# A decoder step in split precision: ScalarE's work on loaded tiles kept in program order, decode steps and operand builds spread over each pair of M tiles

## The chip, the cores and the metric

The kernel runs on one core of a Trainium2 chip. The metric is the device time of one execution in microseconds (us), lower is better. The time before is the median of three runs.

## What is computed

One inference step of a two-layer trunk, for 512 prompt tokens and 8 sample tokens (one new token each, with a state of its own). All 520 tokens go through the same weights; the model width is 2048.

```python
h = rmsnorm(x, norm_g)
z = h @ w_in                       # 2048 -> 8192: B, C, xc, g_conv | q, k, v, g_ret, 1024 columns each
y_conv = B * conv3(C * xc) * silu(g_conv)                 # causal, width 3
q, k = rope(q), rope(k) / 16       # 4 heads of 256
o = retention(q, k, v, S0)         # decayed linear attention, chunks; new state S
y_ret = groupnorm(o) * gn_g * silu(g_ret)
x = x + concat(y_conv, y_ret) @ w_out
x = x + sigmoid(x @ w_pg) * (p @ w_ple)
# after the last layer: rmsnorm(x, final_g)
```

For the 8 sample tokens the retention is a decode step on a 256x256 state of each token and head: S = gamma * S + k^T v, o = q S. The new states are outputs as well. 2 layers x 4 heads x 8 tokens are 64 such steps.

## The kernel before

**Split precision.** Each fp32 operand is held as two parts of the type fp32r: a high part (a copy by ScalarE, line 222 for weights, line 527 for operands) and a low part (the rest, a subtraction by VectorE, lines 223 and 528). Each product is three matmuls, lines 240 to 242: high x high, high x low, low x high. The accumulators are PSUM banks of 260 columns, a half (LEFT or RIGHT) of the 520 tokens.

**Pairs of M tiles.** The four large products (w_in, w_out, w_pg, and w_in of the next layer) are done two M tiles of 128 rows at a time by pair(). For each pair a table (HEADS, CONVS, OUT_ROWS, GATES) gives a number s of the 16 K tiles that go through one step of Strassen's scheme (strassen(): 7 products instead of 8); the rest, from s to 16, is done plainly at the end. s = 0 means two plain products, one after the other (gemm()). In strassen() the products come in this order: `times(a, w11, k1)`, `times(b, w21, t1)`, `times(a, w21, t2)`, `times(d, w12, ...)`, then aside(), `times(a, w11, t3)`, `times(b, w21, ...)`, `times(a, w22, t4)`, then the plain rest, the last copies out of PSUM and a second aside(). Between the first four products VectorE adds weight tiles (line 305). ScalarE copies finished banks (line 293).

**Operands.** An Operands object (X, O, Gt: the input of w_in, w_out and w_pg) holds the split K tiles and, for the first s of them, four split sums per pair of tiles (sums, t1 to t4). build() makes those of one pair: a gain by ScalarE for X (line 455), operand_sums() on VectorE (lines 403 to 406), then split(). The tiles come from HBM through send(), one pair ahead of the build (AHEAD = 1), by the DMA queue of POOL (SIDE), line 1026 or 636. fill(most) builds at most `most` pairs, sending one ahead, as far as slots are free; supply(k) builds what a product needs at once. s grows over the first pairs of each product (0, 4, 8, 12, 14 or 4, 8, 12, 16), so sums must be made while pairs run. Before, MORE_HEAD = MORE_OUT = MORE_GATE = 2 builds are done at the end of each pair; MORE_CONV = 1 after each pair of the convolution stage. free() builds the next set's operands in the last pair of a product, as the old ones go.

**Retention.** head(m) runs a pair of q, k, v or g_ret tiles; steps(h) is a list s0 to s8 of small pieces for a head's prompt tokens, one of which is run at each aside(). two() (line 842) splits a tile that was loaded from scratch in HBM (hs). Decode steps are run by sample(): it finishes the step whose tiles were loaded in the call before (sample_step: ScalarE scales the state, line 747; VectorE adds two outer products, line 751, and reduces twice, line 755; POOL stores the state, line 752) and issues the loads of the next (sample_load: sret, line 741, and kq, line 742). In the head stage, sample() is called once after each pair, and twice after each second one (k and g_ret); in the convolution stage once before each pair.

**Order.** The program is written in one order, but a planner sets the order of each engine's queue: it simulates the run and issues on each engine, of the instructions that are ready by its own clock, the one that comes first in the program. Some stand ahead of their place by high_priority (PSUM copies, and by WPRIO = 20 places the weight splits). On the chip an engine takes its queue strictly as it was laid out. tc.keep_in_program_order(ins) adds an edge, without a wait, from the instruction that was written just before on the same engine: ins cannot be laid out ahead of that one; others can still pass.

Of the kernel before, what the change touches and what calls it, by code (L numbers as in the profile page):

```python
# [9 lines left out]
AF = mybir.ActivationFunctionType  # L10
# [32 lines left out]
RESERVE_NEXT = 10  # L43
AHEAD = 1
PRE = 9
MORE_HEAD, MORE_CONV, MORE_OUT, MORE_GATE = 2, 1, 2, 2
ROOT = (0, 3)
SPREAD = (0, 6)

# [138 lines left out]
def trunk_kernel(  # L188
# [19 lines left out]
    split_ring = Ring(const, SPLIT, F32R, "split")  # L208
    banks = Banks(pg, 5)
    later = []  # L210


    def load(src):
# [62 lines left out]
    def strassen(x, src0, src1, s, step=None):  # L276
# [70 lines left out]
        if c is None:  # L347
            plus(z1[:, RIGHT], a, z1[:, RIGHT])
        else:
            copy(z1[:, LEFT], a)  # L350
        times(b, w21, at(ops, k2, RIGHT), False, True)
        raw_ring.put(w21)
        step(6)
# [26 lines left out]
    def pair(x, src, m, n, nxt=None):  # L380


        s = x.rows[n]
        last = n == len(x.rows) - 1 and nxt is not None
        if s:
            z = strassen(x, src[m], src[m + 1], s, (lambda i: x.free(i, nxt)) if last else None)
        else:
            z0 = gemm(x, src[m], s)
            aside()
            z1 = gemm(x, src[m + 1], s)  # L390
            aside()
            z = z0, z1
            if last:
                x.free(8, nxt)
        x.release(n + 1)
        if nxt is not None and not last and not x.todo:
            nxt.fill(1, PRE)
        return z
# [14 lines left out]
    class Operands:  # L413
# [44 lines left out]
        def fill(self, most=KT, reserve=None):  # L458

            reserve = self.reserve if reserve is None else reserve  # L460
            while self.todo and self.todo[0][0] < self.ready:
# [8 lines left out]
                    continue  # L470
                break

        def supply(self, k):

            while self.todo and self.todo[0][1] and 2 * self.todo[0][0] < k:
                self.build()
# [44 lines left out]
    def split(src, g=None, free_src=True, halves=False, right=True):  # L521
        x, y = getr(), getr() if right else None
        op = Op(x, y, halves)
        for n in ((LEFT, RIGHT) if right else (LEFT,)) if halves else (slice(0, T),):
            hi, lo = op.view(n)
            if g is None:
                S.activation(hi, src[:, n], AF.Copy)  # L527
                V.tensor_tensor(lo, src[:, n], F(hi), SUB)  # L528
            else:
                S.activation(hi, src[:, n], AF.Identity, scale=g)  # L530
                V.scalar_tensor_tensor(lo, src[:, n], g, F(hi), MUL, SUB)  # L531
        if free_src:
            put(src)
        return op
# [153 lines left out]
    for l in range(DEPTH):  # L688
# [55 lines left out]

        def sample_step(h, b, st, kb):

            S.activation(st[:, :512], st[:, :512], AF.Identity, scale=gam(h))  # L747
            k = kb[:, 256:512]
            for e in range(2):
                c = slice(256 * e, 256 * e + 256)  # L750
                V.scalar_tensor_tensor(st[:, c], k, vs[:, h, e, b : b + 1], st[:, c], MUL, ADD)  # L751
            SIDE.dma_start(o_rets[l, h, b], st[:, :512])  # L752
            for e in range(2):
                c = slice(256 * e, 256 * e + 256)
                V.tensor_tensor_reduce(k, st[:, c], kb[:, :256], 1.0, 0.0, MUL, ADD, osum[:, e, h, b : b + 1])  # L755
            put(st, kb)
# [13 lines left out]
        skipped = 2 if l == 0 else 0  # L770

        def head(m):
            zs = pair(X, wi[l], m, m // 2 - skipped)
            X.fill(MORE_HEAD, 0)
            for _ in range(1 + m // 2 % 2):
                sample()
            return zs

        def aside_copy(h, i, tiles):
# [49 lines left out]
        def steps(h):  # L829
# [9 lines left out]

            def two(src, scale=1.0):  # L840
                hi, lo = getr(), getr()
                S.activation(hi[:, :512], src[:, :512], AF.Copy, scale=scale)
                if scale == 1.0:
                    V.tensor_tensor(lo[:, :512], src[:, :512], F(hi[:, :512]), SUB)
                else:
                    V.scalar_tensor_tensor(lo[:, :512], src[:, :512], scale, F(hi[:, :512]), MUL, SUB)
                return hi, lo
# [195 lines left out]
        for j in range(CJ):  # L1043
            mt = 32 + 4 * j
            O.ready = min(j // 2, 3)
            sample()
            zc, zx = pair(X, wi[l], mt, mt // 2 - skipped, O)
            u = get()
            times(u, zc, r2)
# [13 lines left out]
            put(u)  # L1063
            V.tensor_tensor(t, t, rb, MUL)
            X.fill(MORE_CONV, 0)
            sample()
            if j == CJ - 1:
                while loaded or todo:
                    sample()
# [26 lines left out]
        for m in range(0, KT, 2):  # L1096
            xs = [get(), get()]
            for i in range(2):
                SIDE.dma_start(xs[i], res[m + i])
            Gt.ready = m // 2  # L1100
            zs = pair(O, wo[l], m, m // 2, Gt)
            for i, (x, z) in enumerate(zip(xs, zs)):
                for n, v in z:
                    V.tensor_tensor(x[:, n], v, x[:, n], ADD)
                z.done()
                SIDE.dma_start(x1s[l, m + i], x)
                if m < SPILL_X:
                    put(x)
                else:
                    x1[m + i] = x  # L1110
            O.fill(MORE_OUT, 0)


        pops = []
# [24 lines left out]
        for m in range(0, KT - tail, 2):  # L1139
            pes, xs = [], [again(x1s, m), again(x1s, m + 1)]  # L1140
            later.append(lambda m=m, w=parts(wp[l, m // 2], 0, 4), pes=pes: embed(m, w, pes))
            if X:
                X.ready = m // 2
            zs = pair(Gt, wg[l], m, m // 2, X)
            if m == KT - 2:
                put(*pops[0].slots, *pops[1].slots)
            Gt.fill(MORE_GATE, 0)
            for i, z in enumerate(zs):
                x = xs[i]
                for h, (n, ps) in enumerate(zip((LEFT, RIGHT), pes[2 * i : 2 * i + 2])):  # L1150
# [273 lines left out]
```

## Time and profile before

| | before |
|---|---|
| median of 3 runs | 2240.52 us (2238.61 to 2245.47) |
| the profiled execution's own time | 2244.63 us |
| its span, first to last instruction | 2242.9 us |
| mean granted TensorE clock | 0.995 |
| TensorE (PE) busy | 2170.0 us, 97%, 17,854 matmuls |
| VectorE (DVE) busy | 1907.8 us, 85% |
| ScalarE (ACT) busy | 1291.9 us, 58% |
| GpSimd (POOL) busy | 442.6 us, 20% |
| DMA | 392.11 MB, mean 175 GB/s |

A row of waits reads "engine, tile and line of the waiting instruction <- what it waited for: us in all, times, longest". A row of a group reads "line, engine, operation, out<-in, shapes, count | busy us, mean ns of one | idle us of the engine just before, and what ended most of it". Tiles of the pool of slots are all called slot; raw is a loaded weight tile, split its two parts, ps_g a PSUM bank, hs, kq, yc, x1s, x2s and ys are scratch in HBM, sret is the input states.

### The profile page before, as it was taken

The page shows a single profiled execution, that of the slowest core. Times are in us where ns is not written, and L with a number is a line of the kernel's source. Part 1 is how long each engine was busy: PE and PEld are TensorE (multiplying, and loading weights), DVE is VectorE, ACT ScalarE, POOL GpSimd, SP SyncE. Part 2 cuts the span into 40 slices and gives each one's busy share as a digit, 9 for nine tenths or more (in the row PEclk, how much of TensorE's full clock was granted, in tenths as well). Part 3 has the DMA queues.
Part 4 walks back from the last instruction along what each step waited for, and adds up shares of the span by engine and source line. Part 5 has one row for each costly group of instructions (what it writes and reads, how often), then busy time and mean ns, then how long its engine had stood idle before and what let it go on. Part 6 is the DMA issues. An engine that isn't in the chain of part 4 may idle for free. (4 is left out here: it accounts for less than half of the span.)

```text
span 2242.9 us, 48558 instructions
## 1 busy us (share of the span) xinstructions
PE 2170.0 (97%) x17854; PEld 2152.9 (96%) x17854; DVE 1907.8 (85%) x3928; ACT 1291.9 (58%) x2789; POOL 442.6 (20%) x764
## 2 busy tenths in 40 slices
PE   8999999999999899999999999999999999999998
PEld 8999999999999899999989999999999998999998
DVE  8788889889999877887997898889989998788875
ACT  8556455555555645655775555565555565456555
POOL 3213222212010210210212222222121011112011
PEclk9999999999999999999999999999999999999999
DMA  7656565655433754645545466556454355547445
GB/s 266 192 160 193 169 188 186 192 153 184 140 117 120 235 166 152 233 150 173 199 149 186 150 199 190 183 182 201 142 181 131 119 162 194 189 137 252 134 145 200
DMA packets 189072, 392.11 MB, mean 175 GB/s; under 512 B 26720, under 2 KB 69728, under 8 KB 188832
## 3 DMA queue, kind: packets, MB, share of 16 engines
q1 hardware_dynamic: 134336, 214.38, 31.0%
q0 software_dynamic: 54496, 174.62, 23.6%
q8 instruction: 140, 2.29, 0.4%
q14 instruction: 100, 0.82, 0.1%
HBM read 323.74 MB, written 65.15 MB: 173 GB/s over the span
## 5 line engine op out<-in xcount | busy, mean ns | idle before, releaser
L240 PE MATMUL ps_g<-slot,split 128*128 128x260 f32 x5496 | 1550.6, 285 | 53.0 <-ACT split L222 18.0
L241 PE MATMUL ps_g<-slot,split 128*128 128x260 f32 x5496 | 1549.2, 283 | 0.1
L242 PE MATMUL ps_g<-slot,split 128*128 128x260 f32 x5496 | 1539.7, 284 | 4.7 <-DVE split L223 4.6
L222 ACT ACTIVATE split<-raw 128x512 fp32r<-128x512 f32 (+2 forms) x1401 | 783.0, 579 | 568.5 <-DVE raw L305 258.4
L240 PEld LDWEIGHTS ps_g<-slot,split 128*128 128x128 f32 x5496 | 1035.0, 189 | 63.6 <-ACT split L222 21.0
L241 PEld LDWEIGHTS ps_g<-slot,split 128*128 128x128 f32 x5496 | 1039.7, 189 | 0.3 <-DVE slot L531 0.3
L242 PEld LDWEIGHTS ps_g<-slot,split 128*128 128x128 f32 x5496 | 1032.9, 189 | 7.4 <-DVE split L223 7.4
L223 DVE TENSOR_TENSOR split<-raw,split 128x512 fp32r<-128x512 f32 (+2 forms) x1401 | 857.2, 632 | 168.7 <-ACT split L222 93.2
L305 DVE TENSOR_TENSOR raw<-raw 128x512 f32<-128x512 f32 (+2 forms) x688 | 430.2, 637 | 22.2 <-DMA raw<-wi 16.5
L293 ACT ACTIVATE slot<-ps_g 128x260 f32<-128x260 f32 x368 | 137.0, 378 | 110.3 <-PE ps_g L242 98.5
L527 ACT ACTIVATE slot<-slot 128x520 fp32r<-128x520 f32 (+1 forms) x202 | 110.6, 569 | 47.3 <-DVE slot L404 23.3
L528 DVE TENSOR_TENSOR slot<-slot,slot 128x520 fp32r<-128x520 f32 (+1 forms) x202 | 122.5, 624 | 12.4 <-ACT slot L527 12.0
L751 DVE SCALAR_TENSOR_TENSOR slot<-slot,vs,slot 128x256 f32<-128x256 f32 x128 | 56.8, 482 | 41.9 <-DMA slot<-kq 29.8
L293 DVE TENSOR_TENSOR slot<-ps_g,slot 128x260 f32<-128x260 f32 x184 | 77.9, 425 | 5.6 <-PE ps_g L242 5.4
L747 ACT ACTIVATE slot<-slot,vec 128x512 f32<-128x512 f32 x64 | 46.0, 720 | 49.3 <-DMA slot<-sret 46.4
L752 POOL DMA_DIRECT2D o_rets<-slot x64 | 35.4, 553 | 197.4 <-ACT split L222 85.7
L293 ACT ACTIVATE ps_g<-ps_g 128x260 f32<-128x260 f32 x146 | 54.1, 371 | 31.2 <-PE ps_g L242 30.9
L741 POOL DMA_DIRECT2D slot<-sret x64 | 35.1, 549 | 186.2 <-DVE slot L710 29.9
L1026 POOL DMA_DIRECT2D slot<-x1s x82 | 43.9, 538 | 131.1 <-DVE slot L528 31.7
L782 POOL DMA_DIRECT2D hs<-slot x64 | 35.2, 550 | 158.9 <-DVE slot L726 87.6
L837 POOL DMA_DIRECT2D slot<-hs x64 | 46.2, 723 | 63.3 <-PE ps_st L242 23.2
L742 POOL DMA_DIRECT2D slot<-kq x64 | 35.2, 551 | 108.0 <-DVE slot L710 23.8
(213 smaller groups left out, 1686.1 us busy)
## 6 DMA issues: line engine op xcount, KB each, us to landing
raw<-wi SPq DMA_DIRECT2D x377, 256.0 KB, 4.1
raw<-wi SPq DMA_DIRECT2D x136, 192.0 KB, 3.9
raw<-wo SPq DMA_DIRECT2D x96, 256.0 KB, 4.3
raw<-wg SPq DMA_DIRECT2D x88, 256.0 KB, 4.4
slot<-x1s POOLq DMA_DIRECT2D x82, 260.0 KB, 5.6
slot<-sret POOLq DMA_DIRECT2D x64, 256.0 KB, 4.1
hs<-slot POOLq DMA_DIRECT2D x64, 256.0 KB, 3.6
slot<-hs POOLq DMA_DIRECT2D x64, 256.0 KB, 4.7
```

What stands on the lines that cost most here:

```text
L222: S.activation(hi, raw, AF.Copy)
L223: V.tensor_tensor(lo, raw, F(hi), SUB)
L240: PE.matmul(out, wh, xh, start=start, stop=False, skip_group_check=more)
L241: PE.matmul(out, wh, xl, start=False, stop=False, skip_group_check=more)
L242: PE.matmul(out, wl, xh, start=False, stop=stop, skip_group_check=more)
L293: fn(*args)
L305: V.tensor_tensor(out[:, n], x[:, n], y[:, n], op)
L527: S.activation(hi, src[:, n], AF.Copy)
L528: V.tensor_tensor(lo, src[:, n], F(hi), SUB)
L747: S.activation(st[:, :512], st[:, :512], AF.Identity, scale=gam(h))
L751: V.scalar_tensor_tensor(st[:, c], k, vs[:, h, e, b : b + 1], st[:, c], MUL, ADD)
L837: SIDE.dma_start(t[:, :512].rearrange("p (m n) -> p m n", m=2), src)
```

## The change

1. A list `middle` is emptied in strassen() after the fifth product and its copy, and between the two plain products where s = 0.
2. MORE_HEAD, MORE_OUT and MORE_GATE go from 2 to 1, and a second fill of one is put in the middle of each pair of the head stage, of w_out and of w_pg. A new need(n) builds at the pair's end what the next pair's s requires.
3. The decode steps move: in the head stage, where two were called after a pair, one goes to its middle; in the convolution stage they go from before each pair to its middle.
4. keep (keep_in_program_order) is put on the ScalarE copies of split() without a gain and of two(), and in sample_step on the scaling and the two VectorE additions.

```diff
-MORE_HEAD, MORE_CONV, MORE_OUT, MORE_GATE = 2, 1, 2, 2
+MORE_HEAD, MORE_CONV, MORE_OUT, MORE_GATE = 1, 1, 1, 1
@@ trunk_kernel @@
+    middle = []
+    keep = tc.keep_in_program_order
@@ strassen @@
+        while middle:
+            middle.pop(0)()
         times(b, w21, at(ops, k2, RIGHT), False, True)
@@ pair @@
             z0 = gemm(x, src[m], s)
+            while middle:
+                middle.pop(0)()
             aside()
             z1 = gemm(x, src[m + 1], s)
@@ Operands @@
+        def need(self, n):
+            while n < len(self.rows) and len(self.sums) < self.rows[n] // 2:
+                self.build()
@@ split @@
-                S.activation(hi, src[:, n], AF.Copy)
+                keep(S.activation(hi, src[:, n], AF.Copy))
@@ sample_step @@
-            S.activation(st[:, :512], st[:, :512], AF.Identity, scale=gam(h))
+            keep(S.activation(st[:, :512], st[:, :512], AF.Identity, scale=gam(h)))
...
-                V.scalar_tensor_tensor(st[:, c], k, vs[:, h, e, b : b + 1], st[:, c], MUL, ADD)
+                keep(V.scalar_tensor_tensor(st[:, c], k, vs[:, h, e, b : b + 1], st[:, c], MUL, ADD))
@@ head @@
+            middle.append(lambda: X.fill(MORE_HEAD, 0))
+            if m // 2 % 2:
+                middle.append(sample)
             zs = pair(X, wi[l], m, m // 2 - skipped)
             X.fill(MORE_HEAD, 0)
-            for _ in range(1 + m // 2 % 2):
-                sample()
+            X.need(m // 2 - skipped + 1)
+            sample()
             return zs
@@ two @@
-                S.activation(hi[:, :512], src[:, :512], AF.Copy, scale=scale)
+                keep(S.activation(hi[:, :512], src[:, :512], AF.Copy, scale=scale))
@@ convolution stage, pair 1 and 2 of each j @@
-            sample()
+            middle.append(sample)
             zc, zx = pair(X, wi[l], mt, mt // 2 - skipped, O)
...
-            sample()
+            if j < CJ - 1:
+                middle.append(sample)
@@ w_out @@
+            middle.append(lambda: O.fill(MORE_OUT, 0))
             zs = pair(O, wo[l], m, m // 2, Gt)
...
             O.fill(MORE_OUT, 0)
+            O.need(m // 2 + 1)
@@ w_pg @@
+            middle.append(lambda: Gt.fill(MORE_GATE, 0))
             zs = pair(Gt, wg[l], m, m // 2, X)
...
             Gt.fill(MORE_GATE, 0)
+            Gt.need(m // 2 + 1)
```

## The prediction, made before the result was known

> **What bounds the kernel now.** I read the page first, then the table of stretches of 56 us, then the waits by engine, and last the stretches around single stops of TensorE. TensorE bounds it:
>
> ```profile
> span 2242.9 us, 48558 instructions
> PE 2170.0 (97%) x17854; PEld 2152.9 (96%) x17854; DVE 1907.8 (85%) x3928; ACT 1291.9 (58%) x2789; POOL 442.6 (20%) x764
> ...
> 617.00:673.00 56.00, 56.00 (x470) 56.00 (x469) 52.51 (x101) 30.15 (x58) 7.57 (x3) 1.00 0.40 117
> ```
>
> In the third row (length, then busy time and count of PE, PEld, DVE, ACT, POOL, then clock, DMA share, GB/s) TensorE never stops: 56.00 / 470 = 0.119 us per matmul. The 17,854 matmuls would take 2127 us at that pace, so about 116 us of the span are losses, 73 of them plain idle (2242.9 - 2170.0). The change touches no matmul; all it can win lies there. VectorE is the second bound: 52.51 of 56 us busy in that stretch, 94%. What ends TensorE's idle time:
>
> ```profile
> PE ps_g L240 <- ACT split L222: 18.0, 12, 4.6
> PE ps_g L240 <- ACT slot L293: 15.2, 17, 2.0
> PE ps_g L240 <- ACT ps_g L293: 12.6, 11, 2.8
> ...
> PE ps_g L242 <- DVE split L223: 4.6, 11, 0.7
> ```
>
> (us in all, times, longest.) 45.8 us end with ScalarE: with the high part of a weight tile (L222) or with the copy that empties a PSUM bank (L293). These are short instructions that stood behind something in ScalarE's queue. What they stood behind is in the other engines' waits:
>
> ```profile
> ACT slot L747 <- DMA slot<-sret: 46.4, 36, 4.0
> DVE slot L751 <- DMA slot<-kq: 29.8, 12, 5.5
> ACT slot L527 <- DVE slot L404: 23.3, 10, 4.9
> ACT slot L842 <- DMA slot<-hs: 10.3, 5, 3.8
> DVE slot L404 <- DMA slot<-x1s: 8.1, 3, 3.8
> DVE slot L403 <- DMA slot<-yc: 5.8, 2, 3.1
> DVE slot L404 <- DMA slot<-yc: 5.1, 2, 3.1
> ```
>
> Of 64 decode steps, 36 find ScalarE standing at L747 for a state tile still under way: the planner put them just where it believed the tile would land. One such stop in full, in the order of time (start, length, engine, line; in brackets the idle time before):
>
> ```profile
> 265.44 0.28 PE L242 MATMUL ps_g<-slot,split 128*128 128x260 f32 x1
> 267.42 0.63 ACT L842 ACTIVATE slot<-slot 128x512 fp32r<-128x512 f32 x1 [3.84 <-DMA slot<-hs]
> 267.95 0.61 ACT L222 ACTIVATE split<-raw 128x512 fp32r<-128x512 f32 x1
> ...
> 268.62 0.39 PE L240 MATMUL ps_g<-slot,split 128*128 128x260 f32 x1 [2.90 <-ACT split L222]
> ```
>
> ScalarE stands 3.84 us at a retention operand (L842); the weight tile behind it comes late; TensorE is idle for 2.90 us. A stop of this size costs more than its idle time:
>
> ```profile
> 265.20:273.40 8.20, 4.99 (x27) 4.58 (x26) 5.25 (x12) 5.18 (x11) 0.55 (x1) 0.79 0.39 124
> 273.40:281.60 8.20, 8.20 (x71) 8.20 (x71) 6.82 (x13) 4.56 (x11) 1.28 (x2) 1.00 0.52 145
> ```
>
> Over the 8.2 us around it the granted clock is 0.79, so 0.21 x 8.2 = 1.7 us go on top.
>
> **The change part by part.** No instruction is added or taken out; all is order and place.
>
> *Term 1, held steps.* L747, its two L751, L842 and L527 may no longer be issued ahead of the instruction that the program has before them on their engine. Ten stretches of 5 to 7 us hold the stops of TensorE that follow a wait of L747, L751 or L842 for a loaded tile; the first two, one of the others, and their sum:
>
> ```profile
> 254.50:259.50 5.00, 4.64 (x39) 4.44 (x38) 3.58 (x10) 0.69 (x2) 1.86 (x4) 1.00 0.77 246
> 263.50:270.00 6.50, 3.29 (x25) 2.88 (x24) 2.96 (x8) 2.43 (x6) 1.89 (x3) 1.00 0.55 190
> 310.00:317.00 7.00, 6.05 (x50) 5.84 (x49) 4.05 (x10) 0.80 (x2) 3.43 (x8) 1.00 0.70 256
> ...
> sum 56.00, PE 45.69 PEld 42.42 DVE 36.16 ACT 23.59 POOL 16.47; mean PE 4.57 PEld 4.24 DVE 3.62 ACT 2.36 POOL 1.65
> ```
>
> 56.00 - 45.69 = 10.3 us of idle TensorE, out of 86.5 us of waits (46.4 + 29.8 + 10.3): only an eighth of such a wait gets through to TensorE. Whether the waits go depends on the lead of the loads:
>
> ```profile
> slot<-sret POOLq DMA_DIRECT2D x64, 256.0 KB, 4.1
> ...
> slot<-kq POOLq DMA_DIRECT2D x64, 256.0 KB, 4.6
> ...
> slot<-yc POOLq DMA_DIRECT2D x22, 260.0 KB, 5.2
> ```
>
> A pair with s = 14 has (7 products x 7 tiles + 4 x 2) x 3 = 171 matmuls, 20.4 us; the new place in its middle comes after 5 products, 105 matmuls, 12.5 us, and 7.9 us remain. A step was loaded one call of sample() before, so it now has a lead of 7.9 or 12.5 us in the program against a landing of 4.6; in head pairs with two calls it had none, as load and step stood back to back. The load still waits for its turn in POOL's queue, so I take three quarters of 10.3: 7.7 us. The ends are 0 (the stop moves to another place) and 10.3.
>
> *Term 2, the clock.* The stop at 268.6 goes with term 1, and with it 1.7 us. The Trainium skill, page TensorE: Matmul & The Clock Gate, Part 1 (the table of the two states), has the half clock come after an idle window of about 3.4 us; by that rule an idle time of 2.90 us brings none and this term is zero. The rows above have it after 2.90 us, and I go by them.
>
> *Term 3, operand builds, one in the middle and one at the end of each pair instead of two at the end* (X in the head, O, Gt; convolution pairs keep theirs). It acts where operand sums still grow, some 20 pairs. With one pair of tiles sent ahead (AHEAD), the second build of a fill sent its own load and needed it at once; now each load gets half a pair. The two O stretches and one Gt stretch where VectorE stands at L403 or L404 for a tile and TensorE stops behind it:
>
> ```profile
> 806.00:814.00 8.00, 6.71 (x56) 6.50 (x56) 4.38 (x9) 2.59 (x5) 1.08 (x2) 1.00 0.57 197
> ...
> sum 21.50, PE 17.87 PEld 17.24 DVE 10.69 ACT 7.12 POOL 1.68; mean PE 5.96 PEld 5.75 DVE 3.56 ACT 2.37 POOL 0.56
> ```
>
> 21.50 - 17.87 = 3.6 us. L403 to L406 are not held, the planner can still place them at the believed landing, so I take half: 1.8. Ends: 0 and 3.6. The first growth pair of O and Gt gains nothing: end fill plus need() still build two there.
>
> *What the moved steps cost in the middle.* A decode step issues one L747, two L751, two sums (L755) with their accumulator reads, a store and two loads; a build of sums adds two loads, four small operations (L403 to L406) and two splits (L527, L528):
>
> ```profile
> L528 DVE TENSOR_TENSOR slot<-slot,slot 128x520 fp32r<-128x520 f32 (+1 forms) x202 | 122.5, 624 | 12.4 <-ACT slot L527 12.0
> ...
> L751 DVE SCALAR_TENSOR_TENSOR slot<-slot,vs,slot 128x256 f32<-128x256 f32 x128 | 56.8, 482 | 41.9 <-DMA slot<-kq 29.8 <-ACT slot L747 11.8
> ...
> L755 DVE CUSTOM_DVE_ANT_0 slot<-slot,slot 128x256 f32<-128x256 f32 x128 | 53.6, 423 | 0.1
> ...
> L223 DVE TENSOR_TENSOR split<-raw,split 128x512 fp32r<-128x512 f32 (+2 forms) x1401 | 857.2, 632 | 168.7 <-ACT split L222 93.2 <-PE ps_g L241 58.5 <-PE ps_g L242 5.1
> L305 DVE TENSOR_TENSOR raw<-raw 128x512 f32<-128x512 f32 (+2 forms) x688 | 430.2, 637 | 22.2 <-DMA raw<-wi 16.5 <-DMA raw<-wg 1.9
> L293 DVE TENSOR_TENSOR slot<-ps_g,slot 128x260 f32<-128x260 f32 x184 | 77.9, 425 | 5.6 <-PE ps_g L242 5.4
> ```
>
> VectorE before the middle: four additions (L305) of two chunks and ten splits, 8 x 0.637 + 10 x 0.632 = 11.4 of 12.5 us. After it: 6 x 0.632 + 2 x 0.425 = 4.6 of 7.9. So 3.3 us are free there, against 91% busy before; rope, silu and the convolution's elementwise work come after a pair's end, on top of the next pair's additions. A moved step (2 x 0.482 + 2 x 0.423, about 1.8) fits; a build of sums on top of it (4 x 0.43 by L293's size, plus 2 x 0.624, 3.0) overruns by 1.5, in four head pairs that have both (k and g pairs while X grows); the engines' lead over TensorE covers that. If it doesn't, it is 6 us. I take 0. In turn VectorE loses its 29.8 us of standing at L751, in stretches where it is at 94%; an eighth of that, as above, was counted in term 1. On POOL's queue a step's three transfers only change places with hs, ys and yc traffic; POOL is busy for 20%. SP's weight loads keep their order.
>
> *Term 4, what holding costs.* A held split (L527) of a build at a pair's end now comes behind the copy of the last bank. For one build this chain is:
>
> ```profile
> L293 ACT ACTIVATE slot<-ps_g 128x260 f32<-128x260 f32 x368 | 137.0, 378 | 110.3 <-PE ps_g L242 98.5 <-DVE osum L755 5.3 <-DMA hs<-slot 2.8
> ...
> L527 ACT ACTIVATE slot<-slot 128x520 fp32r<-128x520 f32 (+1 forms) x202 | 110.6, 569 | 47.3 <-DVE slot L404 23.3 <-DMA x2s<-slot 4.4 <-DMA slot<-yc 4.0
> ```
>
> 0.38 + 2 x 0.57 + 0.62 = 2.1 us. The next pair reads the new sum as the last of its second product; before it, at s = 8, run 4 + 3 tiles of three matmuls, 2.5 us. So one build is covered, two (0.38 + 4 x 0.57 + 0.62 = 3.3) are 0.8 us late. Two stand only at the end of a first growth pair, five places: 4 us. Part of this the planner also ran that late before; I take half, 2. Ends: a gain of 2.9 (L527's waits for L404, 23.3 us, at one eighth) and a loss of 5 places x 3.3 + 15 x 2.1 = 48 with no cover at all; I stay near the first, as the 2.5 us of matmuls stand ahead of the sum in any order.
>
> **Sum.** 7.7 + 1.7 + 1.8 - 2 = 9.2 us off, on the profiled execution: 2242.9 - 9.2 = 2233.7 of span. That execution's own time is 2244.63, the median of the three runs 2240.52 (2238.61 to 2245.47), so on the median it is 2231.
>
> **The rivals.** *A larger gain.* All of terms 1 and 3 (13.9), the clock, no cost, and the stops at the growth pairs that show no late tile go as well, because builds no longer come in twos. One example:
>
> ```profile
> 748.00:756.20 8.20, 5.46 (x32) 5.46 (x33) 8.11 (x21) 3.69 (x12) 1.07 (x2) 0.79 0.83 253
> 1121.00:1129.20 8.20, 5.48 (x34) 5.49 (x35) 7.83 (x19) 8.20 (x20) 2.13 (x4) 0.79 0.99 367
> ```
>
> Here ScalarE or VectorE is full for nearly the whole stretch. But these two stand where one operand set gives way to the next, and those fills (free) stay as they are. Of the 45.8 us that end with ScalarE, 45.8 - 10.3 - 3.6 = 31.9 belong to no term; with a quarter of them, 13.9 + 1.7 + 8.0 = 23.6 and the time is 2217.
>
> *The stops move.* L885, L403 and L404 keep floating, and each held instruction shifts what is put beside it; weight tiles still come late. For it: an eighth of the waits reaches TensorE, so 86 us of ScalarE and VectorE waits can vanish for little. Against it: the three named tiles head the list of waits for loaded tiles. Time 2240, give or take 5.
>
> *Slower: held splits starve the growth pairs.* At some 20 growth pairs the second product waits for a sum whose splits come only behind the end copy. It costs the chain less half its cover, 2.1 - 1.25 = 0.85 us at 15 places and 3.3 - 1.25 = 2.05 at five, 23 us, plus two half clocks, 3.4. It decides once the weight splits of the next pair, which ScalarE has to do too, take half of the 2.5 us. With term 1's gain left, 2240 + 26 - 9 = 2257; if only half of the places are hit, 2244. Against it: L527 follows its own VectorE work (23.3 us of waiting for L404), so it was rarely early.
>
> **How the numbers follow.** A measurement of this kernel can tell about 0.3%, 6.7 us: faster is below 2233.8, slower above 2247.2. The forecast (2223 to 2236) has 0.43, of which 0.06 lies above 2233.8; the larger gain 0.19, all faster; the stops that move 0.20, of which 0.02 on each side; the slower case 0.18, a third of it below 2247. Faster: 0.37 + 0.19 + 0.02 = 0.58. Slower: 0.12 + 0.02 = 0.14. Within: 0.06 + 0.16 + 0.06 = 0.28. The likeliest time is 2231; its own range is 2223 to 2236. The range for 8 in 10 takes in the larger gain with some room below it and the half-hit slower case, 2214 to 2250.
>
> **What would show it.** Term 1: the waits of L747 for sret and of L751 for kq fall from 46.4 and 29.8 us to below 15 together, L842 for hs to below 4. Term 2: no clock of 0.79 near 268. Term 3: L403 and L404 wait under half as long for x1s and yc. Term 4: TensorE's waits at L240 for a slot (L527, L528) stay absent; if they appear after growth pairs, the slower case holds. PE idle (span less PE busy) falls from 73 to about 65. The prediction is wrong if the idle time ended by L222 and L293 keeps its 45.8 us although the waits for loaded tiles are gone, or if waits of L222 for raw tiles grow in their place.

## The result, and the profile after

The changed kernel takes 2207.65 us (median of 4 runs, 2203.91 to 2211.48); the kernel before, run beside it, 2242.99 (4 runs, 2238.61 to 2249.33). The ratio is 0.984, with a 95% interval of 0.981 to 0.987: 35 us or 1.6% faster. I had forecast 9 us, and a range down to 2214. The sign was right, the forecast gain was a quarter of the real one, and the time lies outside the range. The profiled execution after took 2211.48 us.

The head of the page of after, and below it one stretch of its table (length, busy time and count of PE, PEld, DVE, ACT, POOL, clock, DMA share, GB/s):

```profile
span 2209.7 us, 48509 instructions
PE 2164.1 (98%) x17854; PEld 2153.7 (97%) x17854; DVE 1906.0 (86%) x3928; ACT 1291.3 (58%) x2789; POOL 443.1 (20%) x764
...
617.00:673.00 56.00, 56.00 (x470) 56.00 (x469) 53.04 (x106) 30.89 (x63) 2.17 (x4) 1.00 0.41 125
```

The undisturbed pace is what it was, 470 matmuls in 56 us. The work is the same on every engine; TensorE's idle time went from 72.9 to 45.6 us (span less PE busy). Where the rest went shows when I cut the span at the stages. What a stage loses is its length less its matmuls at 56.00 / 470 us each, which takes in idle time, half clocks and slow matmuls together. First the kernel before: head, convolution and w_out of the first layer, then of the second:

```profile
45.00:427.00 382.00, 374.70 (x3095) 372.19 (x3095) 325.63 (x724) 217.81 (x483) 104.67 (x178) 1.00 0.59 183
427.00:735.00 308.00, 299.60 (x2474) 296.77 (x2473) 277.46 (x547) 170.29 (x353) 43.99 (x65) 1.00 0.47 144
735.00:912.00 177.00, 167.85 (x1374) 166.40 (x1374) 144.27 (x278) 95.71 (x214) 31.76 (x60) 0.99 0.56 183
...
1113.00:1537.00 424.00, 409.22 (x3356) 404.94 (x3355) 365.27 (x805) 248.28 (x552) 107.41 (x185) 0.99 0.58 183
1537.00:1841.00 304.00, 298.56 (x2473) 296.41 (x2473) 277.66 (x548) 169.85 (x347) 40.75 (x60) 1.00 0.47 145
1841.00:2019.00 178.00, 170.54 (x1399) 169.28 (x1398) 145.82 (x280) 95.51 (x211) 32.47 (x61) 0.99 0.55 181
```

The same six stages after:

```profile
45.00:414.00 369.00, 367.67 (x3061) 366.56 (x3061) 321.05 (x710) 217.90 (x475) 102.96 (x175) 1.00 0.58 185
414.00:719.00 305.00, 303.56 (x2534) 303.02 (x2533) 279.47 (x560) 172.66 (x360) 45.37 (x69) 1.00 0.49 152
719.00:894.00 175.00, 167.81 (x1354) 166.27 (x1352) 145.30 (x280) 94.39 (x217) 31.02 (x59) 0.97 0.56 182
...
1098.00:1504.00 406.00, 400.40 (x3322) 398.82 (x3321) 362.25 (x794) 247.67 (x544) 102.90 (x177) 1.00 0.59 186
1504.00:1806.00 302.00, 301.38 (x2514) 301.06 (x2513) 278.71 (x556) 170.91 (x350) 44.92 (x65) 1.00 0.49 152
1806.00:1985.00 179.00, 172.79 (x1402) 171.03 (x1401) 149.07 (x288) 97.94 (x219) 33.73 (x63) 0.98 0.57 188
```

Take the first row of each: 382.00 - 3095 x 0.11915 = 13.2 us lost before, 369.00 - 3061 x 0.11915 = 4.3 after. (The number of matmuls differs a little because the cuts are made at transfers.) All of them, in us, the sums from unrounded values:

| stage | before | after |
|---|---|---|
| head, layer 0 + layer 1 | 13.2 + 24.1 = 37.4 | 4.3 + 10.2 = 14.5 |
| convolution | 13.2 + 9.3 = 22.6 | 3.1 + 2.5 = 5.5 |
| w_out | 13.3 + 11.3 = 24.6 | 13.7 + 12.0 = 25.6 |
| all else: the start, w_pg, the end | 31.1 | 36.8 |

So the whole gain sits in the head and the convolution stages, where the decode steps run: 40 us there, of which some 7 are lost again in the other two rows. The last row is the rest of the span's loss: before 2242.9 - 17,854 x 0.11915 = 115.6 in all, after 82.4, so 33.2 in the two profiles. A second profile of the changed kernel, taken with the last experiments, gives 13.7, 5.8, 27.5 and 31.6: differences of 2 us in the first three rows and of 5 in the last mean nothing. Between two kernels the planner's order differs as well, and a stage that an edit leaves alone can move with it: w_out has no decode step, and two kernels further down that differ from the one before in the decode steps alone lose 15.4 and 14.8 us there against 24.6.

What ends TensorE's idle time, after (us in all, times, longest):

```profile
PE ps_g L243 <- ACT ps_g L296: 13.6, 7, 4.6
PE ps_g L243 <- ACT slot L296: 8.4, 11, 3.6
PE ps_g L243 <- ACT slot L542: 6.0, 2, 5.3
PE ps_g L243 <- DVE slot L296: 2.3, 2, 2.0
PE ps_g L243 <- ACT split L225: 2.0, 4, 0.6
```

Lines have moved: L222, L293, L403, L404, L747, L751 and L842 of before are L225, L296, L410, L411, L759, L763 and L857 here. The waits for a weight split fell from 18.0 us to 2.0, and the two rows of the bank copy L296 for ScalarE from 27.8 to 22.0. Waits of L759 for sret (46.4 before), of L763 for kq (29.8) and of L857 for hs (10.3) are not in the list any more at all.

### The profile page after: what moved, and what is told of

The parts are those of the page before. It is cut to its first block, busy times and chain, and to the rows that moved or that the text cites. A ratio compares the mean times of both kernels' runs of the same rounds, so it can differ in the third digit from the quotient of the medians.

```text
span 2209.7 us, 48509 instructions
## 1 busy us (share of the span) xinstructions
PE 2164.1 (98%) x17854; PEld 2153.7 (97%) x17854; DVE 1906.0 (86%) x3928; ACT 1291.3 (58%) x2789; POOL 443.1 (20%) x764
## 5 line engine op out<-in xcount | busy, mean ns | idle before, releaser
L243 PE MATMUL ps_g<-slot,split 128*128 128x260 f32 x5496 | 1549.8, 285 | 33.0 <-ACT ps_g L296 13.6
L225 ACT ACTIVATE split<-raw 128x512 fp32r<-128x512 f32 (+2 forms) x1401 | 785.1, 580 | 624.6 <-DVE raw L308 206.7
L226 DVE TENSOR_TENSOR split<-raw,split 128x512 fp32r<-128x512 f32 (+2 forms) x1401 | 848.1, 627 | 185.4 <-ACT split L225 116.6
L296 ACT ACTIVATE slot<-ps_g 128x260 f32<-128x260 f32 x368 | 139.0, 380 | 123.4 <-PE ps_g L245 105.9
L540 DVE TENSOR_TENSOR slot<-slot,slot 128x520 fp32r<-128x520 f32 (+1 forms) x202 | 118.6, 616 | 4.6 <-ACT slot L539 4.0
L539 ACT ACTIVATE slot<-slot 128x520 fp32r<-128x520 f32 (+1 forms) x202 | 104.8, 570 | 11.4 <-DMA slot<-x1s 3.1
L764 POOL DMA_DIRECT2D o_rets<-slot x64 | 35.4, 553 | 344.2 <-DVE slot L763 132.9
L296 DVE TENSOR_TENSOR slot<-ps_g,slot 128x260 f32<-128x260 f32 x184 | 77.3, 421 | 7.6 <-PE ps_g L245 4.6
L296 ACT ACTIVATE ps_g<-ps_g 128x260 f32<-128x260 f32 x146 | 54.4, 373 | 20.7 <-PE ps_g L245 20.3
L763 DVE SCALAR_TENSOR_TENSOR slot<-slot,vs,slot 128x256 f32<-128x256 f32 x128 | 55.9, 477 | 8.6 <-ACT slot L759 8.5
L722 DVE TENSOR_TENSOR slot<-slot,slot 128x520 f32<-128x520 f32 x80 | 55.3, 691 | 7.6 <-DMA o_rets<-slot 7.0
```

Of the source, the lines that this page charges most:

```text
L225: S.activation(hi, raw, AF.Copy)
L226: V.tensor_tensor(lo, raw, F(hi), SUB)
L243: PE.matmul(out, wh, xh, start=start, stop=False, skip_group_check=more)
L296: fn(*args)
L539: keep(S.activation(hi, src[:, n], AF.Copy))
L722: V.tensor_tensor(out[:, n], v, table[:, n], MUL)
```

## The experiments

All runs of a group stood beside the kernel before on one chip; ratios are to it. Losses by stage are worked out as above, from one profile of each kernel.

### The change taken apart

**Holding alone** (before, with the keeps, no step moved):

```diff
+    keep = tc.keep_in_program_order
-                S.activation(hi, src[:, n], AF.Copy)
+                keep(S.activation(hi, src[:, n], AF.Copy))
...
+            keep(S.activation(st[:, :512], st[:, :512], AF.Identity, scale=gam(h)))
+                keep(V.scalar_tensor_tensor(st[:, c], k, vs[:, h, e, b : b + 1], st[:, c], MUL, ADD))
+                keep(S.activation(hi[:, :512], src[:, :512], AF.Copy, scale=scale))
```

> The kernel before with the holding alone (split, two, sample_step); decode steps and builds stay at the ends of the pairs. Theory A (the waits for loaded tiles themselves cost the 35 us, by way of the weight splits queued behind them): the waits of L747 and L751 for sret and kq fall below 15 us together and the time comes to 2207 to 2220. Theory B (the place counts: VectorE's crowded first half of a pair is relieved): 2230 to 2243, the gain is in the moves. Theory C (the spread of the operand builds counts): 2230 to 2243 as well.

Measured: 2229.46 us, 0.9931 (0.9905 to 0.9956), 15 us faster, just below what B and C gave and 9 us above A. Its waits for the step's tiles, and then its first head and first convolution stage:

```profile
DVE slot L752 <- DMA slot<-kq: 8.8, 6, 3.1
ACT slot L748 <- DMA slot<-sret: 4.5, 3, 1.9
```

```profile
45.00:428.00 383.00, 370.71 (x3050) 367.00 (x3050) 319.90 (x708) 212.81 (x471) 104.22 (x176) 1.00 0.57 180
428.00:730.00 302.00, 302.00 (x2525) 302.00 (x2524) 279.62 (x550) 172.69 (x356) 40.13 (x57) 1.00 0.47 148
```

The waits are nearly gone (13.3 of 76.2 us left), and in the convolution stage TensorE does not stop once in 302 us. The head loses as much as before (35.9 of 37.4; its first layer even more, 19.6 against 13.2), although the waits are gone there too. The w_out stages lose 29.8, 5 more than before.

**Moves alone** (after, with all keeps taken off):

```diff
-                keep(S.activation(hi, src[:, n], AF.Copy))
+                S.activation(hi, src[:, n], AF.Copy)
```

and the same in sample_step and two().

> The changed kernel with no instruction held; builds and decode steps are spread as in it. Theory A: the planner again puts L747 and L751 where it believes the tiles land, their waits stay at 50 us or more, the time 2228 to 2243. Theory B: 2207 to 2220. Theory C: 2207 to 2220.

Measured: 2218.43 us, 0.9892 (0.9857 to 0.9927), 26 us faster. Its waits for the same tiles:

```profile
ACT slot L759 <- DMA slot<-sret: 75.2, 40, 5.7
DVE slot L763 <- DMA slot<-kq: 26.8, 15, 5.1
ACT slot L857 <- DMA slot<-hs: 15.9, 10, 3.9
```

118 us of waits, more than the 86.5 before, in a kernel that is 26 us faster. That settles one thing: the sum of these waits does not measure what they cost. That each costs what stands behind it on its queue without slack is my reading of it, not shown. The head loses 31.1 us here, the convolution 7.5.

**Decode steps back at the ends, the rest as after:**

```diff
-            if m // 2 % 2:
-                middle.append(sample)
...
-            sample()
+            for _ in range(1 + m // 2 % 2):
+                sample()
...
-            middle.append(sample)
+            sample()
             zc, zx = pair(X, wi[l], mt, mt // 2 - skipped, O)
```

and likewise for the second pair of each j.

> The changed kernel with the decode steps back at the ends of pairs (head stage) and before each pair (convolution stage); builds spread, all held. Theory A: at most 10 us lost, 2207 to 2218, through loads that follow their step too closely in head pairs with two steps. Theory B: 2225 or more. Theory C: 2205 to 2212.

Measured: 2224.21 us, 0.9909 (0.9884 to 0.9935), a little below theory B and above A. The head loses 35.4 us, the convolution 2.8. The two head stages:

```profile
45.00:427.00 382.00, 370.89 (x3055) 368.78 (x3056) 320.62 (x711) 213.40 (x473) 104.86 (x178) 0.99 0.57 181
...
1106.00:1520.00 414.00, 404.11 (x3329) 400.75 (x3329) 364.69 (x800) 246.98 (x545) 105.67 (x181) 0.99 0.58 185
```

**Builds back at the ends** (two fills there, none in the middle, the rest as after):

```diff
-MORE_HEAD, MORE_CONV, MORE_OUT, MORE_GATE = 1, 1, 1, 1
+MORE_HEAD, MORE_CONV, MORE_OUT, MORE_GATE = 2, 1, 2, 2
-            middle.append(lambda: X.fill(MORE_HEAD, 0))
-            middle.append(lambda: O.fill(MORE_OUT, 0))
-            middle.append(lambda: Gt.fill(MORE_GATE, 0))
```

> The changed kernel with two builds at the end of each pair as before; decode steps spread, all held. Theories A and B: 2205 to 2212, as the changed kernel. Theory C: 2225 or more.

Measured: 2210.8 us, 0.9847 (0.9821 to 0.9874): the same as the change (0.984). Spreading the builds is worth nothing that these runs can tell.

What follows from the four: in the convolution stage either half is enough (2.6 lost with holding, 7.5 with the moves, 22.6 with neither). In the head each half alone leaves 31 to 36 of 37.4 us, and only both together bring 14.5.

### Which hold

Each from after, with the named keeps taken off.

**The operand splits free:**

> The changed kernel with split() not held (L527 of before); two() and the decode steps stay held. Theory D (holding the operand splits costs time where operand sums grow, in w_out above all: 26 to 30 us are lost there in the kernels that hold them against 16 without): w_out's loss in both layers falls from 26 to about 16 us and the time to 2194 to 2202. Rival (the 16 us of the kernel without holding come from elsewhere in the order): 2204 to 2214.

Measured: 2204.22 us, 0.9822 (0.9799 to 0.9846), against 0.984 of the change: some 3 us better if anything. Theory D did not come true: w_out loses 23.0 us, not 16. The intervals overlap; the two are told apart below.

**The decode step free** (the scaling and both additions):

> The changed kernel with the decode steps not held, two() and split() held. If holding the decode steps is what makes the head stage even (loss 14 us in both layers against 31 with nothing held): the head stage loses 25 us or more and the time is 2218 to 2230. If it is two() that counts: 2205 to 2213.

Measured: 2232.53 us, 0.9946 (0.9926 to 0.9965): 25 us of the 35 gone. The second head stage of this kernel loses 424.00 - 3333 x 0.11915 = 26.9 us, more than before (24.1); below it the kernel's waits for the step's tiles:

```profile
1100.00:1524.00 424.00, 406.18 (x3333) 402.48 (x3331) 361.94 (x800) 245.11 (x543) 105.23 (x180) 0.99 0.56 180
```

```profile
ACT slot L759 <- DMA slot<-sret: 81.1, 41, 5.0
DVE slot L763 <- DMA slot<-kq: 38.6, 19, 6.5
```

**two() free:**

> The changed kernel with two() not held, the rest held. If the decode steps are what counts: 2205 to 2213, with waits of two() for hs of 10 us or more. If two() counts: the head stage loses 25 us or more, 2218 to 2230.

Measured: 2219.6 us, 0.9887 (0.9862 to 0.9912): 12 us gone, 10 of them in the head (24.5 lost against 14.5).

**The additions that make operand sums held as well, their splits free.** If holding what waits for a loaded tile is good as such, L410 to L412 should be held too:

```diff
-        V.tensor_tensor(a[:, LEFT], f0[:, RIGHT], f0[:, LEFT], SUB)
+        keep(V.tensor_tensor(a[:, LEFT], f0[:, RIGHT], f0[:, LEFT], SUB))
```

and the next two likewise.

> The changed kernel with split() not held (2204 us) and instead the first three subtractions of each operand sum held on VectorE, where the waits for x1s and yc remain. If these waits stop TensorE in the growth pairs: w_out and w_pg lose 40 us or less together instead of 45, 2195 to 2202. Otherwise 2202 to 2212.

Measured: 2237.07 us, 0.9962 (0.9947 to 0.9977), far from both expectations: most of the gain is lost again, and 33 us against the kernel with the splits alone free. What the table above calls all else loses 56.7 us against 34.1 there; 7 of the difference are in the first w_pg stage (13.5 against 6.3). The weight splits are late once more:

```profile
PE ps_g L243 <- ACT split L225: 19.7, 13, 5.2
```

Against 2.0 us in after, and 18.0 before. So holding what waits for a loaded tile is not good as such. My reading, from this one kernel: holding is good for a step that has slack of its own, and a sum that the next pair needs has none.

### What is wrong with the end of a pair in the head

With everything held, all decode steps at the ends cost 13 us against the changed places by the kernel beside them (2224.21 and 2210.8, builds at the ends) and 17 by the change's own median (2207.65), all of it in the head. The changed kernel still calls one step at the end of every head pair, two steps out of three; only the second one of each second pair has moved. So one step at the end does no harm that shows, and two do. I tried what they could collide with.

**The middle, but earlier or later:** the list is emptied after the second product, among VectorE's four weight additions, or after the sixth, past them.

```diff
         copy(z1[:, RIGHT] if c is None else c, b)
+        while middle:
+            middle.pop(0)()
```

(early; late has the two lines ahead of `times(a, w22, t4, ...)`. In both, and in the kernels below that move the list, the two lines at the old place go.)

> The changed kernel with the middle work (one decode step, one build) called after the second product of a pair instead of the fifth; all held. Theory B1a (VectorE is crowded by weight additions in the first four products): the head and convolution stages lose 30 us or more together, 2220 to 2235. Theory B1b (what counts is to be away from the ends of pairs, where rope, silu and the retention pieces stand): 2204 to 2214.

> The changed kernel with the middle work called after the sixth product; all held. B1a: 2203 to 2211, the additions are over there too. B1b: between, 2207 to 2218, as it comes nearer to the end of the pair.

Measured: 2209.6 us, 0.9838 (0.9815 to 0.9861), and 2208.01 us, 0.9832 (0.9808 to 0.9855). Both are the same as the change. So VectorE's additions before the fifth product, by which I had worked out 3.3 us of free time after it, do not decide.

**Both steps of a pair in the middle, back to back:**

```diff
-            if m // 2 % 2:
+            for _ in range(1 + m // 2 % 2):
                 middle.append(sample)
...
-            sample()
```

> The changed kernel with all decode steps of the head stage in the middle of their pair: in each second pair two back to back, the second with its load just issued. Theory B1 (the place counts: the end of a pair and the start of the next are crowded on VectorE): the head stage stays near 14 us of loss, 2203 to 2213. Theory B2 (two steps back to back count, as the second has no lead for its load, wherever they stand): the head stage goes back to about 34 us, 2222 to 2232.

Measured: 2207.43 us, 0.9835 (0.9808 to 0.9862), the same. Two steps in a row, the second with no lead at all for its loads, cost nothing in the middle, and with no step left at the ends nothing more is won.

**Behind the retention piece**, just before the fifth product:

```diff
         aside()
+        while middle:
+            middle.pop(0)()
         times(a, w11, t3, False, True)
```

> The changed kernel with the middle work called right behind the retention piece of the pair's middle, before the fifth product; all held. If it is the retention pieces that a held step must not stand behind: 2216 to 2228. Theories E and F: 2204 to 2213, as any place inside the pair.

Measured: 2205.22 us, 0.9835 (0.9807 to 0.9863). So standing behind a piece of retention, the neighbour at the pair's end, is not the trouble either.

**Just before the next pair** instead of just after the old one, so behind the rope and silu work that stands between them; two in a row before each second pair:

```diff
         def head(m):
+            for _ in range(1 + m // 2 % 2):
+                sample()
...
-            if m // 2 % 2:
-                middle.append(sample)
...
-            sample()
```

> The changed kernel with the head stage's decode steps called just before the next pair, after rope and silu of the last one, instead of after and in the middle of a pair; all held. Theory E (a held step at the end is laid out among rope, silu and the pieces of the retention that the pair's end calls, ahead of rope in the program; VectorE does that cluster before the next pair's weight parts): here the steps come behind rope in the program, the head stage loses about 14 us as in the changed kernel, 2204 to 2214. Theory F (the boundary itself is bad, on either side of rope): 2218 to 2228.

Measured: 2216.94 us, 0.9878 (0.9853 to 0.9904). Some 7 us better than at the old end and 9 worse than in the middle, between the two theories; the head loses 26.7 us.

**Steps at the end, their reductions cut to 8 columns** (the sample tokens' retention output is left out with that; one of the two reductions is shown):

```diff
-                V.tensor_tensor_reduce(k, st[:, c], kb[:, :256], 1.0, 0.0, MUL, ADD, osum[:, e, h, b : b + 1])
+            V.tensor_tensor_reduce(k[:, :8], st[:, :8], kb[:, :8], 1.0, 0.0, MUL, ADD, osum[:, 0, h, b : b + 1])
```

> The kernel with the decode steps at the ends of pairs, all held (2224 us), with each of the two reductions of a decode step cut from 256 columns to 8, so that the sample tokens' retention output is left out; stores and loads as before. If VectorE's crowding at the ends is what the moves relieve: 50 us less of VectorE work there bring back most of the 16 us, 2206 to 2215. If it is the order of POOL's stores and loads there: 2220 to 2228.

Measured: 2219.75 us, 0.9879 (0.985 to 0.9907), 4 us below the same kernel with whole reductions by the times (2224.21, in another group), 7 by the ratios, whose intervals overlap, and still 10 to 12 above the two kernels beside it that have the steps in the middle. The head loses 32.7 us against 35.4. The cut is smaller than I had expected: a reduction of 8 columns still takes 160 ns against 417, so 33 us of VectorE's work go and not 50, out of 109 in all the steps. This run alone does not rule VectorE's work out.

The effect does not look like an accident of the planner's order: in the seven profiles with everything held and never two steps at the end of a pair the head loses 10.7 to 16.5 us, in the five with two there, held or not, and their loads in place 32.7 to 39.6. What the boundary of a pair does to the second step stays open. It is neither the end alone, where one step does no harm, nor two steps in a row alone, nor a piece of retention ahead of them. The next two kernels narrow it down: with the steps as before, two at each second end and unheld, but without their loads, the head loses only 13.6 us, with all of the steps' work on VectorE and ScalarE still there. So what costs there is the loads and what waits for them, not the steps' work as such.

### Before, without the loads

**Decode steps that read a resident tile; their 128 loads are left out**, and with them the right states and sample outputs. The additions and reductions read the resident tile in place of kq too (not shown):

```diff
-            SIDE.dma_start(st[:, :512], sret[l, h, b])
-            SIDE.dma_start(kb[:, :512], kq[l, h, b].rearrange("c d -> (c d)").partition_broadcast(P))
...
-            S.activation(st[:, :512], st[:, :512], AF.Identity, scale=gam(h))
+            S.activation(st[:, :512], rb[:, :512], AF.Identity, scale=gam(h))
```

> The kernel before, with the decode steps reading a resident tile, and their two loads left out (64 states and 64 kq tiles; the sample tokens' retention output and states are left out so). No wait for sret or kq can stand. If these waits cost the time (the prediction's term 1, whatever the factor): 2205 to 2220. If the order on VectorE and ScalarE costs it: 2228 to 2242.

Measured: 2198.89 us, 0.9802 (0.978 to 0.9824): 45 us faster than before, with no step held or moved, and below even the first expectation. The head loses 13.6 us and the convolution 4.5, as much as in the changed kernel; another 9 us came off in w_out (15.4). The two head stages:

```profile
45.00:409.00 364.00, 363.38 (x3033) 362.68 (x3032) 319.85 (x712) 215.96 (x473) 78.16 (x129) 1.00 0.49 155
...
1083.00:1496.00 413.00, 407.09 (x3374) 404.91 (x3373) 367.64 (x809) 254.64 (x558) 84.26 (x141) 1.00 0.49 159
```

413.00 - 3374 x 0.11915 = 11.0 us are lost in the second, against 24.1 before.

**The same, with the loads issued into tiles that nobody reads:**

```diff
+            put(st, kb)
+            return h, b
+        def sample_step(h, b):
+            st, kb = get(), get()
```

> As the kernel without the loads of the decode steps (2199 us), but with both loads issued at their old place into tiles that nothing reads; states and kq are left out of the results. If the waits were what cost: 2198 to 2212, there are none here. If it was the loads' traffic (64 x 512 KB) and their place in POOL's queue: 2225 to 2243.

Measured: 2230.33 us, 0.9924 (0.9905 to 0.9942): 17 us faster than before, some 30 slower than without the loads. Its two head stages:

```profile
45.00:420.00 375.00, 367.07 (x3046) 364.71 (x3045) 320.59 (x714) 214.67 (x471) 106.39 (x177) 1.00 0.58 184
...
1095.00:1520.00 425.00, 408.03 (x3336) 404.00 (x3334) 364.21 (x805) 250.45 (x548) 108.97 (x187) 0.99 0.57 182
```

The step reads nothing of its loads here, but whoever gets the slot next still waits for the transfer, the step itself included. ScalarE and VectorE still stand 47.6 us for sret and kq, against 76.2 before, so my expectation that no such wait is left did not hold, and this kernel does not part the waits from the loads' traffic. What it shows: the loads with all that hangs on them cost some 45 us in the kernel before, of which about 17 go when the step does not read them. Those came off in the convolution (13.1 lost) and w_out (14.8); the head loses 39.6, as before. How the other 28 divide between slots, POOL's queue and traffic, this pair does not tell.

### The best of the pieces

**Behind the retention piece, operand splits free**, beside the changed kernel:

```diff
         aside()
+        while middle:
+            middle.pop(0)()
         times(a, w11, t3, False, True)
...
-                keep(S.activation(hi, src[:, n], AF.Copy))
+                S.activation(hi, src[:, n], AF.Copy)
```

> The middle work behind the retention piece, split() not held, two() and the decode steps held: the two edits that came out lowest. If both count: 2196 to 2203, below the changed kernel in the same call by more than its interval. If they were chance: within 4 us of it.

> The changed kernel once more, to stand beside the one above on the same chip: 2204 to 2211.

Measured: 2199.59 us (2196.35 to 2201.22), 0.9783 (0.9768 to 0.9799); the changed kernel 2207.61 (2204.34 to 2212.03), 0.9823 (0.9805 to 0.9841). The version beats the change by 8 us, 0.36%, and no run of the one lies among those of the other. The page of its profile:

```profile
span 2199.4 us, 48568 instructions
PE 2156.8 (98%) x17854; PEld 2147.4 (98%) x17854; DVE 1906.4 (87%) x3928; ACT 1295.2 (59%) x2789; POOL 444.1 (20%) x764
```

Its w_out loses 20.0 us against 27.5 in the changed kernel beside it, its head and convolution 13.6 and 3.6 against 13.7 and 5.8. Held operand splits thus cost w_out some 7 us here. The other kernels agree: in w_out the 13 profiles with held splits lose 24.2 to 31.4 us, the six with splits and sums free 14.8 to 24.6.

## Why the prediction was right and wrong

**The reading of the bound was right.** TensorE bounds, the pace of 0.119 us per matmul stayed, and all of the gain came from its losses.

**Term 1, held steps: the step that failed is its size, "only an eighth of such a wait gets through to TensorE".** I counted the stops of TensorE that stand directly behind a wait for a loaded tile, 10.3 us in ten stretches, and took 7.7. The head and convolution stages together lost 60.0 us before and 20.0 after: 40 us, four times all that I had counted. The mechanism was right in part. In the convolution, holding alone takes the waits and the loss away (22.6 to 2.6). In the head it takes the waits away and the loss stays (35.9 of 37.4); there the place of the second step decides as well, to which I had given nothing beyond the lead of its loads. Holding alone came out at 2229, next to my 2231, but by luck: it won 20.0 us in the convolution and 1.5 in the head, and gave back 5 in w_out.

In the first convolution stage alone 13.2 were lost; the stops with no such wait in front of them were my 31.9 us that "belong to no term". This is one of them, in the kernel before, TensorE and then ScalarE:

```profile
574.16 0.39 PE L240 MATMUL ps_g<-slot,split 128*128 128x260 f32 x1 [1.95 <-ACT split L222]
...
573.48 0.63 ACT L222 ACTIVATE split<-raw 128x512 fp32r<-128x512 f32 x1 [2.66 <-DMA raw<-wi]
```

By its row it is a late weight tile and has nothing to do with decode steps. Yet with holding alone the stage shows no stop at all (302.00 busy of 302.00). How a wait for a state tile makes a weight tile late some pairs on no run isolates. The trace before the stop points at a backlog on VectorE: it is busy for 18.2 of the 18.2 us from 556.00 to 574.20, and from 540 to 575 SP's weight loads stand 41 us for raw tiles that VectorE has not yet read (L223, L305). What is shown is that the price of the disorder can't be read off the stops next to its cause. The larger gain that I had as a rival gave a quarter of those 31.9 us and was still 9 us short.

The forecast of the waits was right: those of the three tiles, 86.5 us, are gone (forecast: below 19). My reason, the lead of the loads, was not what took most of them away: with everything held and the steps back at the ends, where two still stand back to back, 11.9 us are left. And that they were gone could not have told the time: with holding alone they fall to a sixth for 15 us, with moves alone they grow for 26.

**Term 2, the clock: right in its place, nothing in the sum.** The window at 268 runs through at full clock, but half clocks stand elsewhere (0.97 in the first w_out stage against 0.99 before), and over the whole span the mean granted clock is 0.994 against 0.995:

```profile
265.00:273.00 8.00, 8.00 (x69) 8.00 (x69) 6.51 (x15) 7.15 (x16) 1.15 (x2) 1.00 0.41 120
```

**Term 3, builds spread, 1.8 us: nothing was gained.** Without it the time is the same (2210.8, 0.9847). L410 and L411 wait less for x1s and yc, 12.6 us against 23.2 of L403 and L404, though not under half as I had put it (the prediction's 8.1, 5.8 and 5.1, and the first row here, of before; the others are of after):

```profile
DVE slot L403 <- DMA slot<-x1s: 4.2, 3, 1.8
```

```profile
DVE slot L411 <- DMA slot<-x1s: 6.6, 2, 4.6
DVE slot L410 <- DMA slot<-x1s: 4.6, 2, 3.5
...
DVE slot L411 <- DMA slot<-yc: 1.4, 1, 1.4
```

and w_out loses 25.6 us as it did 24.6. Again waits went and time did not.

**The moved steps at no cost: right in the result, wrong in its reason.** I took the place after the fifth product for good because VectorE has 3.3 us free there. The places after the second and the sixth are as good. What I did not see is that two steps at the end of a pair were bad: moving one of them away is worth 13 to 17 us on top of holding. That, too, belongs to the size that failed.

**Term 4, a cost of 2 us for the held splits: right in sign, too small.** Freeing them gains some 3 us by itself, within the intervals; 8 with the other place, which alone is worth some 2 (2205.22), and those two differ clear of noise (0.9783 against 0.9835). My sign for the slower case, waits of TensorE for L527 or L528 (L539, L540 here) in the large products, stayed absent in after; the cost came without it.

**Idle time.** I forecast 65 us of idle TensorE; it is 45.6. The part ended by L222 and L293 did not keep its 45.8 us: the three rows of L225 and L296 for ScalarE now make 24.0. Nor did the waits of L222 for raw tiles grow in their place, my other sign of being wrong: wi, wo and wg make 94 us before and 95 after.

## What to carry to other kernels

On an engine that takes its queue in the order laid out (ScalarE at 265 to 268 us, where a weight tile stood behind L842), an instruction that waits for a transfer and that a planner was free to put at the moment the transfer should land can cost far more than the stops beside it, here 40 us against 10: sum what the whole stage loses against its own undisturbed pace, not the waits that have a name. Hold such steps in program order where they have slack, and leave free those that the next product needs (here held operand splits cost 3 to 8 us, held operand sums 33). Test a hold and a place apart and together: here either was enough in one stage, and neither without the other in the next.

## What the runs showed of the hardware

TensorE's clock was halved after shorter stops than I had thought. In after, around 881 us:

```profile
873.00:878.00 5.00, 5.00 (x44) 4.95 (x42) 0.41 (x3) 0.00 (x0) 0.00 (x0) 1.00 0.44 142
878.00:881.00 3.00, 1.00 (x9) 0.84 (x8) 2.93 (x9) 1.39 (x4) 0.00 (x0) 1.00 0.00 0
881.00:884.50 3.50, 3.50 (x19) 3.50 (x18) 3.50 (x9) 2.49 (x8) 0.53 (x1) 0.51 0.00 0
884.50:888.00 3.50, 3.50 (x31) 3.50 (x30) 3.50 (x9) 3.50 (x9) 1.70 (x5) 1.00 0.87 209
```

TensorE is idle for 2.00 of 3.00 us; then it runs 19 matmuls in 3.50 us where 29 fit, at a clock of 0.51, and is at full clock again in the next row. The dip costs 3.50 - 19 x 0.11915 = 1.2 us on top of the 2.00. In the kernel before, the stop at 574, of 1.95 us, has none behind it, and one of 1.91 us at 1461 has one, so the length of the stop alone does not decide:

```profile
574.20:577.70 3.50, 3.50 (x29) 3.50 (x30) 3.44 (x9) 2.39 (x5) 0.00 (x0) 1.00 0.86 228
...
1461.12 0.53 PE L240 MATMUL ps_g<-slot,split 128*128 128x260 f32 x1 [1.91 <-ACT ps_g L293]
...
1461.30:1464.80 3.50, 3.50 (x18) 3.50 (x19) 3.50 (x8) 1.34 (x4) 0.02 (x1) 0.53 0.31 97
```

The Trainium skill, page TensorE: Matmul & The Clock Gate, Part 1, gives an idle window of about 3.4 us for the way down and as long a busy one for the way up, both counted in windows that run freely. The length of the dip agrees (one row of 3.50 us at half clock). If an idle window means one that is idle throughout, the way down does not agree, as TensorE was busy for a third of the 3.00 us ahead of the dip.
